# Sixteen weight-sum transfers behind one timing copy in the first projection

## The chip, the cores and the metric

The kernel runs on one core of one Trainium2 chip. The metric is the device time of one execution in microseconds; of several runs the median is given. The core has a matrix engine (TensorE, PE), a vector engine (VectorE, DVE), a scalar engine (ScalarE, ACT), a general engine (GpSimd, POOL) and a queue engine (SyncE, SP) that issues transfers. Each works through its own instructions strictly in order, and waits for the others by semaphores. Transfers are issued from the queues of SP and POOL and carried out by 16 DMA engines.

## The reference

Two layers over 1024 tokens of width 1024, in float32. Each has a token mixer and a SwiGLU channel mixer of width 2816, with RMS norms before them and residual sums behind. Only the first mixer is touched here:

```python
def short_conv_mixer(h, w_in, conv_w, w_out):
    bcx = h @ w_in                          # 1024 x 3072
    b_gate, c_gate, xv = jnp.split(bcx, 3, axis=-1)
    u = b_gate * xv
    y = depthwise causal convolution of u, 3 taps
    return (c_gate * y) @ w_out             # 1024 x 1024
...
x = x + mix
x = x + (silu(g) * u) @ w_down[i]           # g, u = rmsnorm(x) @ w_gate_up[i]
```

## The kernel before

**Products.** Every float32 operand is split into two parts, a rounded one (hi, made by ACT, L1002) and the rest (lo, made by DVE, L1003), and three matmuls take the place of one. Around that lies a scheme with seven products in place of eight: operands and weights are cut into quadrants, sums of quadrants are formed beforehand, and the seven products, numbered k = 0 to 6, are combined by ACT copies and DVE additions. Products 0, 1 and 4 use plain quadrants of the weights; products 2, 3, 5 and 6 use sums of quadrants (s1 to s4).

**The first projection.** It is computed in ten units (`plan_`), each of two blocks of 128 output columns: "bx" units give a column block of b_gate and one of xv, which are multiplied and go through the three taps, and "cc" units give two blocks of c_gate. One product of one unit is a granule of 12 matmuls. Units 0 to 3 (GROUP = 4) go together, product by product, in the order k = 0, 1, 6, 5, 2, 3, 4; their weight sums were stored ahead. Units 4 to 9 ("direct") go one after the other, in the order k = 2, 5, 3, then k = 0 of the next unit, then k = 4, 6, and k = 1 of the next; their weight sums are formed by DVE on the way. In a unit, tile `sa` takes products 0 and 1 in its first half and 2 and 6 in its second, and `s3` takes product 3. ACT copies the first product of each from its accumulator (L600, L611, L618); DVE adds the others (L588) and then multiplies `sa` by `s3` in place (L644); ACT starts the taps (L549) and DVE adds them (L554).

**Weight sums by transfer.** The second product of this mixer (`w_out`) and the first four units of the channel mixer's first product (`w_gu`) need sums of weight quadrants too. Those are formed without any engine: `sums_by_transfer` makes 16 transfers for each, from DRAM to DRAM, 512 KB each; eight copy a quadrant, and eight add another to it on the way (`accum_op`), L992. They are put into one list of 32: eight copies for `out_sums` (tile name s3, printed s_126), eight copies for `first_sums[0]` (s_0_124), eight additions for the first, eight additions for the second. All go out on the queue of POOL. Their readers come later: the second product loads the sums at L1040 and, for some granules, adds them by transfers of its own on POOL (L1070), and POOL stores the residual stream (L842).

**Order of the work.** A helper `Line` holds the matmuls in a row and puts every other step at a due time: `at(t, f)` runs `f` when the row of matmuls reaches `t`. The instructions of each engine go out in that order and stay in it. A transfer from DRAM to DRAM has no operand that is ready late, so by itself POOL would issue it at once. To give it a place, `transfer_behind` (L672) puts a timing copy ahead of it on POOL: it reads one column of a tile that was written at that point of the row, and writes it to an unused column of `cst`. POOL can't go on until that tile is written; and, the other way round, whoever wants to overwrite the tile waits until POOL has read it. The call stands in `unit_product` at L604, and takes a tile by the number of the product.

Of the kernel before, what the change touches and what calls it, by code (L numbers as in the profile page):

```python
# [46 lines left out]
C_ROOM = 368  # L47
# [14 lines left out]
GROUP = 4  # L62
# [12 lines left out]
def trunk_kernel(ctx: ExitStack, tc: tile.TileContext, xT, small, table, w_in, w_out, w_kv, w_q, w_o, w_gu, w_dn, out):  # L75
# [3 lines left out]
    dve, act, pool, pe = nc.vector, nc.scalar, nc.gpsimd, nc.tensor  # L79
# [3 lines left out]
    def slot(tag, shape=(P, D), dtype=F32, bufs=1):  # L83
        uid[0] += 1
        return sb.tile(list(shape), dtype, tag=tag, name=f"{tag}_{uid[0]}", bufs=bufs)
# [136 lines left out]
    cst = slot("cst", (P, C_ROOM))  # L222
# [128 lines left out]
    def conv_layer():  # L351
# [33 lines left out]
        for k in range(NK):  # L385
# [6 lines left out]
            if k < 2 or k % 2 == 0:  # L392
                n = 1 if k < 2 else 2
# [15 lines left out]
        at = line.at  # L409
# [45 lines left out]
        def sources(u):  # L455
            kind, j = plan_[u]
            m1, m2 = (j, 2 * NK + j) if kind == "bx" else (NK + j, NK + j + 1)
            return w_in[m1], w_in[m2]
# [48 lines left out]
        for p in range(4):  # L507
            t = -3.2 + 1.4 * p
            at(t, scale, 0, 2 * p)
            put(0, p, part(p, 0, 0), t + 0.7)  # L510
            t = 10.0 + 1.5 * p
            at(t, scale, 0, 2 * p + 1)
            put(1, p, part(p, 1, 0), t + 0.7)
            t = 18.5 + 1.7 * p
            at(t, scale, 1, 2 * p + 1)
            put(6, p, part(p, 1, 1), t + 0.7)
            t = 27.0 + 3.4 * p
# [3 lines left out]
            t = 39.2 + 2.6 * p  # L521
            at(t, t_sum, t2(p), part(p, 1, 1), part(p, 0, 0))
            put(2, p, t2(p), t + 1.2)
            t = 49.0 + 2.6 * p
            at(t, t_sum, part(p, 0, 1), part(p, 1, 1), part(p, 0, 1))
            put(3, p, part(p, 0, 1), t + 0.7)
            t = 60.0 + 2.6 * p
# [13 lines left out]
        def taps(j, h, u_of, t):  # L541

            w = [cst[:, C_CONV + i * NK + j : C_CONV + i * NK + j + 1] for i in range(NCONV)]
            c = halves[h]

            def first():
                if h == 0:
                    Y[j] = slot(f"X{j}")
                act.activation(Y[j][:, c], u_of()[:, c], AF.Copy, scale=w[2])  # L549

            def add(s):
                a = max(c.start, s)
                y = Y[j][:, a : c.stop]
                dve.scalar_tensor_tensor(y, u_of()[:, a - s : c.stop - s], w[2 - s], y, ALU.mult, ALU.add)  # L554

            at(t, first)
            at(t + 0.8, add, 1)
            at(t + 0.85, add, 2)
# [5 lines left out]
        def unit_product(u, k, tag, direct):  # L564
            kind, j = plan_[u]
            name = {0: "a", 1: "b1", 2: "a", 3: "a", 4: "a", 5: "b", 6: "b" if direct else "b6"}[k]
            get = bank_at(u, name, tag)
            start = k in (0, 1, 5) or k == 6 and not direct
            ops_of = lambda: B[k]
            w1, w2 = sources(u)  # L570
            if not direct:
                src = {0: w1[:, 0], 1: w1[:, 1], 4: w2[:, 1]}
                src = src[k] if k in src else in_sums[u][SUMS[k]]
                ring_granule(4, ops_of, 0, get, start, True, src=src)
            else:
                raw_of = {
                    0: lambda: units[u, "w1"][:, 0],
                    1: lambda: units[u, "w1"][:, 1],
                    4: lambda: units[u, "w2"][:, 1],
                }  # L580
                ring_granule(4, ops_of, 0, get, start, True, raw_of=raw_of.get(k) or (lambda: units[u, "s", k]))
            t = line.end

            def sa(i):
                return units[u, "sa"][:, halves[i]]

            def add(x):
                dve.tensor_tensor(x(), get(), x(), ALU.add)  # L588

            s3 = lambda: units[u, "s3"]  # L590
            flat = lambda: units[u, "sa"]

            def c22():
                dve.tensor_tensor(s3(), units[u, "b"], s3(), ALU.add)

            if k == 0:

                def f():
                    units[u, "sa"] = slot(sa_tags[u])
                    act.copy(sa(0), get())  # L600

                at(t + 0.05, f)
            if (k in (0, 2, 3, 6) if direct else k in (6, 5, 2, 3)):
                at(t + 0.8, lambda: transfer_behind(transfers, s3() if k in (5, 3) else sa(min(k, 1))))  # L604
            if k == 1:
                at(t + 0.05, add, lambda: sa(0))
                if kind == "cc" and direct:
                    at(t + 0.8, gate, j, 0, lambda: sa(0))
            if k == 2:
                if direct:  # L610
                    at(t + 0.05, lambda: act.copy(sa(1), get()))  # L611
                else:
                    at(t + 0.05, add, lambda: sa(1))
            if k == 3 and direct:

                def f():
                    units[u, "s3"] = slot(f"s{u % 2}", (P, HALF))
                    act.copy(s3(), get())  # L618

                at(t + 0.05, f)  # L620
                at(t + 0.75, c22)
                if kind == "cc":
                    at(t + 2.5, gate, j + 1, 1, s3)
            if k == 3 and not direct:
                at(t + 0.05, add, s3)
                if kind == "bx":
                    at(t + 0.8, lambda: dve.tensor_tensor(sa(1), s3(), sa(1), ALU.mult))
            if k == 5 and not direct:

                def f():  # L630
                    if u in (2, 3):
                        units[u, "s3"] = X[2 * u - 2 - 2 * (u == 2)][:, lo_half]
                    else:
                        units[u, "s3"] = slot(f"s{u % 2}", (P, HALF))
                    act.copy(s3(), get())

                at(t + 0.05, f)
                at(t + 0.1, add, lambda: sa(1))
            if k == 6 and not direct:
                at(t + 0.05, lambda: act.copy(sa(1), get()))  # L640
            if k == 6 and direct:
                at(t + 0.05, add, lambda: sa(1))
                if kind == "bx":
                    at(t + 0.8, lambda: dve.tensor_tensor(sa(1), s3(), sa(1), ALU.mult))  # L644
                    taps(j, 1, flat, t + 2.7)
                else:
                    at(t + 0.8, gate, j, 1, lambda: sa(1))
            if k == 4:
                if kind == "bx":
                    at(t + 0.05, lambda: dve.tensor_tensor(sa(0), get(), sa(0), ALU.mult))  # L650
                    taps(j, 0, flat, t + 1.8)
                    if not direct:
                        taps(j, 1, flat, t + (2.5, 8.0, 10.0)[u])
                elif direct:
                    at(t + 0.05, gate, j + 1, 0, get)
                else:
                    c3 = lambda: X[6][:, lo_half]
                    at(t + 0.05, lambda: act.copy(c3(), get()))

                    for h in (0, 1):  # L660
                        at(t + 9.5, gate, j, h, lambda h=h: sa(h))
                        at(t + 12.5, gate, j + 1, h, (c3, s3)[h])

        for k in (0, 1, 6, 5, 2, 3, 4):
            for u in range(GROUP):
                unit_product(u, k, "acc" if k in (0, 2, 3, 4) else f"P{u % 2}", False)
        group_end = line.end
        transfers = sums_by_transfer(out_sums, w_out[0:NK:2], w_out[1:NK:2])
        more = sums_by_transfer(first_sums[0], w_gu[0, 0:GROUP], w_gu[0, NF : NF + GROUP])
        transfers = deque(transfers[:8] + more[:8] + transfers[8:] + more[8:])  # L670

        def transfer_behind(transfers, src):  # L672
            if transfers:
                pool.tensor_copy(cst[:, C_ROOM - 1 :], src[:, 0:1])
                transfers.popleft()()


        def unit_weights(u, t):
# [26 lines left out]
            for i, d in ((1, 5.8), (2, 5.45), (3, 5.2)):  # L705
                at(t - d * unit, lambda i=i: it["f"][i]())

        steady = lambda u, k: unit_product(u, k, {1: "P1", 5: "P0", 6: "P0"}.get(k, "acc"), True)
        steady(GROUP, 0)
        steady(GROUP, 1)  # L710
# [29 lines left out]
        t = group_end  # L740
# [150 lines left out]
    class Line:  # L891
# [8 lines left out]
        def at(self, t, f, *args):  # L900
            self.n += 1
            heapq.heappush(self.heap, (t, self.n, f, args))
# [79 lines left out]
    def sums_by_transfer(dst, w1, w2):  # L982

        rows = lambda ap: ap.rearrange("u p c -> p u c")
        s3, s4, s1, s2 = (rows(dst[:, i]) for i in range(4))
        a11, a12, a21, a22 = (rows(w[:, :, e]) for w in (w1, w2) for e in (0, 1))
        plan = [(s3, a11), (s1, a21), (s2, a22), (s4, a12), (s3, a21), (s1, a22), (s2, s3), (s4, s2)]
        steps = []
        for i, (to, of) in enumerate(plan):
            how = {"accum_op": ALU.add} if i > 3 else {}  # L990
            for h in (slice(0, 2), slice(2, 4)):
                steps.append(lambda to=to[:, h], of=of[:, h], how=how: nc.gpsimd.dma_start(to, of, **how))  # L992
        return steps
# [1481 lines left out]
```

## Time and profile before

| | |
|---|---|
| runs shown | 1896.95, 1896.89, 1899.06 us; median 1896.95 |
| profiled execution | 1898.37 us, span of its instructions 1896.7 us |
| PE | 1878.8 us busy, 99% of the span |
| DVE | 1351.3 us, 71% |
| ACT | 871.9 us, 46% |
| POOL | 377.5 us, 20% |
| DMA | 368.18 MB, mean 194 GB/s |
| granted clock of PE | 0.996 on average |

The times in the rows are microseconds from the start of the span. Lines such as L674 are lines of the kernel before; in the kernel after the change the same statements stand one or two lines lower. In a row of a timeline the number in front is the start, the next the length, and the brackets hold the idle time before it and what ended that. SPq, POOLq and the like are the sequencers of the engines.

### The profile page before, as it was taken

To read this page: it belongs to the slowest core of one execution; us is meant where nothing else is said; L and a number is where in the kernel's file an instruction comes from. 1 tells how busy PE (TensorE), PEld (TensorE's weight loads), DVE (VectorE), ACT (ScalarE), POOL (GpSimd) and SP (SyncE) were. 2 spreads that over 40 slices of the span, in tenths; PEclk is the share of its full clock that TensorE was granted. 3 is DMA by queue.
4 is the path that set the end of the run, shared out by engine and by line. 5 is a ranking of instruction groups with operands and counts; after the bars stand their busy time and mean duration, and the time that the engine had idled before them with its cause. 6 is when DMAs were issued, how large, how long until landed. Compare 5 with 4: busy or idle time off the path is not lost.

```text
span 1896.7 us, 24889 instructions
## 1 busy us (share of the span) xinstructions
PE 1878.8 (99%) x8518; PEld 1560.3 (82%) x8518; DVE 1351.3 (71%) x2197; ACT 871.9 (46%) x1746; POOL 377.5 (20%) x700
## 2 busy tenths in 40 slices
PE   9998999999999999999999999999999999999999
PEld 7886788888888888888888888888888888888887
DVE  8995797868777777676677888567767666765543
ACT  5542356743333334344566777445333333344441
POOL 0132102212222322000015776400111111100000
PEclk9999999999999999999999999999999999999999
DMA  8776657756666666987741114844454654587563
GB/s 311 236 224 154 122 190 190 185 174 205 214 226 221 228 211 213 354 299 267 232 150 32 25 32 150 319 170 143 146 189 150 220 183 163 163 289 258 198 228 102
DMA packets 173312, 368.18 MB, mean 194 GB/s; under 512 B 17216, under 2 KB 63680, under 8 KB 173056
## 3 DMA queue, kind: packets, MB, share of 16 engines
q1 hardware_dynamic: 138240, 255.78, 40.6%
q0 software_dynamic: 34656, 110.64, 18.8%
q8 instruction: 67, 1.10, 0.2%
q14 instruction: 61, 0.50, 0.1%
q10 hardware_dynamic: 288, 0.16, 0.0%
HBM read 261.26 MB, written 115.87 MB: 199 GB/s over the span
## 4 chain that ended last, share of the span: by engine, by line
PE 94%; DVE 3%; issue 2%; POOL 1%; ACT 0%; POOLq 0%; DVEq 0%; ACTq 0%
PE acc L1086 48%; PE P L1086 28%; PE P L1803 2%; PE P L1805 2%; PE P L1804 2%; PE twin L2030 2%; PE acc L179 1%; PE acc L2110 1%; PE P L1212 1%; PE P L1213 1%; PE P L1211 1%; PE acc L1211 1%; PE acc L1212 1%; PE acc L1213 1%; PE acc L2079 1%
## 5 line engine op out<-in xcount | busy, mean ns | idle before, releaser
L1086 PE MATMUL acc<-XS,G 128*128 128x512 f32 x2568 | 607.1, 391 | 13.1 <-ACT G L611 8.6
L1086 PEld LDWEIGHTS acc<-XS,G 128*128 128x128 f32 x2568 | 485.2, 189 | 115.0 <-ACT G L611 9.1
L1086 PE MATMUL acc<-A,G 128*128 128x512 f32 x1674 | 395.4, 389 | 0.0
L1086 PEld LDWEIGHTS acc<-A,G 128*128 128x128 f32 x1674 | 314.3, 188 | 65.3
L1086 PE MATMUL P<-XS,G 128*128 128x512 f32 x1320 | 311.7, 389 | 0.0
L1086 PEld LDWEIGHTS P<-XS,G 128*128 128x128 f32 x1320 | 247.8, 188 | 51.7 <-ACT G L1362 0.2
L1086 PE MATMUL P<-A,G 128*128 128x512 f32 (+1 forms) x1164 | 273.5, 388 | 0.1
L1086 PEld LDWEIGHTS P<-A,G 128*128 128x128 f32 x1164 | 217.8, 188 | 45.5 <-DVE G L588 0.5
L1003 DVE TENSOR_TENSOR G<-WL,G 128x512 fp32r<-128x512 f32 x168 | 115.8, 690 | 78.3 <-ACT G L1002 77.9
L1002 ACT CAST G<-WR 128x512 fp32r<-128x512 f32 (+1 forms) x210 | 126.9, 605 | 66.7 <-PE acc L1086 27.8
L1003 DVE TENSOR_TENSOR G<-WR,G 128x512 fp32r<-128x512 f32 (+1 forms) x210 | 142.2, 677 | 8.7 <-ACT G L1002 8.7
L1002 ACT CAST G<-WH 128x512 fp32r<-128x512 f32 (+1 forms) x168 | 101.1, 602 | 83.0 <-PE acc L1086 31.6
L1002 ACT CAST G<-WL 128x512 fp32r<-128x512 f32 x168 | 103.6, 617 | 68.2 <-DVE WL L924 63.1
L1003 DVE TENSOR_TENSOR G<-WH,G 128x512 fp32r<-128x512 f32 (+1 forms) x168 | 113.3, 674 | 7.2 <-ACT G L1002 7.1
L1362 ACT ACTIVATE G<-G 128x512 f32<-128x512 f32 x48 | 30.4, 632 | 154.5 <-DVE G L1448 154.5
L1559 DVE TENSOR_TENSOR X<-X,acc 128x512 f32<-128x512 f32 x39 | 26.7, 686 | 87.4 <-PE acc L1086 87.4
L951 POOL DMA_DIRECT2D s<-X x48 | 36.6, 763 | 252.2 <-DVE X L926 124.8
L1443 POOL DMA_DIRECT2D h<-X x44 | 24.5, 558 | 251.4 <-DVE X L1440 244.2
L1429 ACT COPY s<-acc 128x512 f32<-128x512 f32 x40 | 23.5, 587 | 98.3 <-PE acc L1086 98.3
L1448 DVE TENSOR_TENSOR G<-P,G 128x512 f32<-128x512 f32 x40 | 27.6, 689 | 42.2 <-PE P L1086 42.2
L1422 DVE TENSOR_TENSOR s<-P,s 128x512 f32<-128x512 f32 x40 | 27.5, 687 | 35.0 <-ACT s L1429 29.3
L1419 ACT COPY G<-acc 128x512 f32<-128x512 f32 x44 | 25.8, 587 | 57.7 <-PE acc L1086 57.7
(329 smaller groups left out, 2730.3 us busy)
## 6 DMA issues: line engine op xcount, KB each, us to landing
G<-h SPq DMA_DIRECT2D x70, 512.0 KB, 5.0
h<-X POOLq DMA_DIRECT2D x44, 512.0 KB, 5.5
X<-in_w_dn SPq DMA_DIRECT2D x80, 256.0 KB, 3.5
s<-X POOLq DMA_DIRECT2D x40, 512.0 KB, 3.8
WR<-in_w_gu SPq DMA_DIRECT2D x36, 512.0 KB, 5.7
WH<-in_w_gu SPq DMA_DIRECT2D x36, 512.0 KB, 6.5
h<-X POOLq DMA_DIRECT2D x66, 256.0 KB, 3.8
WR<-s SPq DMA_DIRECT2D x64, 256.0 KB, 3.4
```

The lines of the kernel that those rows point to most:

```text
L951: nc.gpsimd.dma_start(dst[:, :, c].rearrange("s p c -> p s c"), it["s"])
L1002: lambda: act.copy(out_hi, raw),
L1003: lambda: lo_eng.tensor_tensor(out_lo, raw, plain(out_hi), ALU.subtract),
L1086: pe.matmul(ps, w[:, wp, c], x[:, xp, q], start=first and i == 0, stop=last and i == 2, skip_group_check=True)
L1211: pe.matmul(ps, hi[:, kc], xs[:, 0, c], start=k == 0, stop=False, skip_group_check=True)
L1212: pe.matmul(ps, hi[:, kc], xs[:, 1, c], start=False, stop=False, skip_group_check=True)
L1213: pe.matmul(ps, lo[:, kc], xs[:, 0, c], start=False, stop=k == n_op - 1, skip_group_check=True)
L1362: state["silu"] = act.activation(x, x if of is None else of, AF.Silu, scale=sign)
L1803: pe.matmul(ps, x[:, 0, t], hi, start=k == 0, stop=False)
L1804: pe.matmul(ps, x[:, 0, t], lo, start=False, stop=False)
L1805: pe.matmul(ps, x[:, 1, t], hi, start=False, stop=k == NK - 1)
L2030: pe.matmul(ps, q, k, start=e == 0, stop=e == 1)
```

## The change

Before, each of 32 steps of the projection put one timing copy and one transfer on POOL: products 6, 5, 2 and 3 of units 0 to 3 (16 steps), then products 0, 2, 3 and 6 of the direct units until the list was empty. After, the first 16 steps are as they were. At product 0 of unit 4 one timing copy is followed by all 16 remaining transfers, and the later products of the direct units issue none.

```diff
-            if (k in (0, 2, 3, 6) if direct else k in (6, 5, 2, 3)):
-                at(t + 0.8, lambda: transfer_behind(transfers, s3() if k in (5, 3) else sa(min(k, 1))))
+            if not direct and k in (6, 5, 2, 3):
+                at(t + 0.8, lambda: transfer_behind(s3() if k in (5, 3) else sa(1), 1))
+            if u == GROUP and k == 0:
+                at(t + 0.8, lambda: transfer_behind(sa(0), 16))
...
-        def transfer_behind(transfers, src):
-            if transfers:
-                pool.tensor_copy(cst[:, C_ROOM - 1 :], src[:, 0:1])
+        def transfer_behind(src, n):
+            pool.tensor_copy(cst[:, C_ROOM - 1 :], src[:, 0:1])
+            for _ in range(n):
                 transfers.popleft()()
```

On POOL, in the middle of the direct units, the instructions before are these (tile names with their buffer: G8, G9 and s1 are buffers of `sa` and `s3` tiles, s3_126 and s1_0_124 the weight sums in DRAM; in brackets the semaphores, where DMASW are those of POOL's transfers):

```order
L674 COPY cst_2_64<-G8_218_1423 128x1 [waits Activation_49,Pool_49]
L992 DMA s3_126<-s3_126 128x2x512 [waits DMASW5_49,DMASW1_49]
L674 COPY cst_2_64<-s1_233_1546 128x1 [waits DVE_49,Pool_49]
L992 DMA s3_126<-s3_126 128x2x512 [waits DMASW2_49,DMASW0_49]
L674 COPY cst_2_64<-G9_235_1566 128x1 [waits Activation_49,Pool_49]
L992 DMA s3_126<-s3_126 128x2x512 [waits DMASW3_49,DMASW1_49]
L674 COPY cst_2_64<-G8_218_1423 128x1 [waits DVE_49,Pool_49]
L992 DMA s1_0_124<-in_w_gu 128x2x512
```

After the change the same transfers stand there without copies, from the one copy of unit 4 on to POOL's next own work, the store at L844:

```order
L675 COPY cst_2_64<-G11_206_1316 128x1 [waits Activation_49,Pool_49]
L994 DMA s3_126<-in_w_out 128x2x512 [waits DMASW4_49]
L994 DMA s3_126<-in_w_out 128x2x512 [waits DMASW5_49]
L994 DMA s3_126<-in_w_out 128x2x512 [waits DMASW6_49]
L994 DMA s3_126<-in_w_out 128x2x512 [waits DMASW7_49]
L994 DMA s3_126<-s3_126 128x2x512 [waits DMASW4_49,DMASW0_49]
...
L994 DMA s1_0_124<-s1_0_124 128x2x512 [waits DMASW2_49,DMASW0_49]
L994 DMA s1_0_124<-s1_0_124 128x2x512 [waits DMASW3_49,DMASW1_49]
L844 DMA xres0_108<-A2_301_2076 128x512 [waits DMAHW1_49,DVE_49]
```

The transfers kept their order and their waits for one another; the waits for ACT and DVE between them went.

On DVE nothing is moved, but what an instruction waits for differs. Unit 5, the end of its products 6 and the multiplication of `sa` by `s3`, before:

```order
L588 TENSOR_TENSOR G_218_1423<-P_228_1503,G_218_1423 128x512 [waits PE_49,Pool_49]
L644 TENSOR_TENSOR G_218_1423<-s_233_1546,G_218_1423 128x512 [waits Pool_49]
L1003 TENSOR_TENSOR G_243_1613<-WH_1436,G_243_1613 128x512 [waits Activation_49]
L588 TENSOR_TENSOR G_235_1566<-P_241_1606,G_235_1566 128x512 [waits PE_49]
L554 SCALAR_TENSOR_TENSOR X_239_1597<-G_218_1423,cst_64,X_239_1597 128x512 [waits Activation_49]
```

And after:

```order
L588 TENSOR_TENSOR G_218_1434<-P_228_1510,G_218_1434 128x512 [waits PE_49]
L646 TENSOR_TENSOR G_218_1434<-s_233_1551,G_218_1434 128x512 [waits DVE_49]
L1005 TENSOR_TENSOR G_243_1614<-WH_1445,G_243_1614 128x512 [waits Activation_49]
L588 TENSOR_TENSOR G_235_1569<-P_241_1607,G_235_1569 128x512 [waits PE_49]
L554 SCALAR_TENSOR_TENSOR X_239_1598<-G_218_1434,cst_64,X_239_1598 128x512 [waits Activation_49]
```

The two places where DVE overwrites `sa` no longer wait for POOL.

## The prediction

> **What bounds the kernel now.** I read the page first, then who waits for whom on TensorE (PE), and then the timelines of single engines around the places where PE waits.
>
> ```profile
> span 1896.7 us, 24889 instructions
> PE 94%; DVE 3%; issue 2%; POOL 1%; ACT 0%; POOLq 0%; DVEq 0%; ACTq 0%
> ```
>
> The chain that ended last is PE for 94% of the span: the kernel is a stream of matmuls, and only what leaves PE idle or slow can be won back. The waits of PE in the first projection and the stages behind it, us 60 to 420, are two (group, total us, times, longest us):
>
> ```profile
> PE acc L1086 <- ACT G L611: 8.6, 1, 8.6
> PE acc L1086 <- ACT s L618: 4.5, 1, 4.5
> ```
>
> Their places stand in PE's timeline (start us, length us, the group, and in brackets the idle time before it). The groups here are 12 matmuls, one granule of one unit:
>
> ```profile
> 128.59 2.88 PE L1086 MATMUL acc<-A,G 128*128 128x512 f32 x12
> 131.31 2.88 PE L1086 MATMUL P<-A,G 128*128 128x512 f32 x12
> ...
> 174.83 2.88 PE L1086 MATMUL P<-A,G 128*128 128x512 f32 x12
> 186.36 5.38 PE L1086 MATMUL acc<-XS,G 128*128 128x512 f32 x12 [8.64 <-ACT G L611]
> 191.57 2.89 PE L1086 MATMUL acc<-A,G 128*128 128x512 f32 x12
> ...
> 230.12 2.88 PE L1086 MATMUL acc<-A,G 128*128 128x512 f32 x12
> 237.50 5.40 PE L1086 MATMUL acc<-XS,G 128*128 128x512 f32 x12 [4.50 <-ACT s L618]
> 242.75 2.92 PE L1086 MATMUL P<-XS,G 128*128 128x512 f32 x12
> ...
> 267.27 5.60 PE L1086 MATMUL acc<-A,G 128*128 128x512 f32 x24
> ```
>
> A group takes 131.31 - 128.59 = 2.72 us when nothing is wrong. After each wait the first group takes 191.57 - 186.36 = 5.21 and 242.75 - 237.50 = 5.25 us. The granted clock says why (windows: us, busy of PE, PEld, DVE, ACT, POOL with instructions, then clock, DMA share, GB/s):
>
> ```profile
> 180.00:190.00 10.00, 3.64 (x9) 2.87 (x10) 6.10 (x14) 2.23 (x4) 2.90 (x4) 0.56 0.66 138
> 230.00:240.00 10.00, 5.50 (x20) 4.16 (x19) 7.74 (x13) 2.95 (x6) 2.50 (x3) 0.79 0.49 82
> ```
>
> So an idle PE also loses its clock for a while: 0.56 and 0.79 of full speed over these ten microseconds.
>
> Now what PE waited for, first place, all engines:
>
> ```profile
> 182.49 1.15 POOL L992 DMA_DIRECT2D s<-s  x1 [4.76 <-issue]
> 183.18 0.65 POOL L674 COPY cst<-G 128x1 f32<-128x1 f32 x1
> 183.87 0.69 DVE L644 TENSOR_TENSOR G<-s,G 128x512 f32<-128x512 f32 x1 [13.37 <-POOL cst L674]
> 184.59 0.72 ACT L549 ACTIVATE X<-G,cst 128x512 f32<-128x512 f32 x1 [15.76 <-DVE G L644]
> 185.73 0.57 ACT L611 COPY G<-acc 128x512 f32<-128x512 f32 x1
> ...
> 186.36 2.08 PE L1086 MATMUL acc<-XS,G 128*128 128x512 f32 x4 [8.64 <-ACT G L611]
> ```
>
> Read it upwards. PE waits for ACT to empty an accumulator (L611). ACT stands in its own order behind the first tap (L549), which waits for VectorE (DVE). DVE's multiplication L644 overwrites a tile, and waits 13.37 us because a timing copy on POOL (L674), which only reads one column of that tile, has not run. The copy stands behind a transfer that POOL could not issue before 182.49. The second place has the same shape:
>
> ```profile
> 231.50 0.66 POOL L674 COPY cst<-G 128x1 f32<-128x1 f32 x1
> 232.19 0.69 DVE L588 TENSOR_TENSOR G<-P,G 128x512 f32<-128x512 f32 x1 [10.36 <-POOL cst L674]
> ...
> 236.87 0.58 ACT L618 COPY s<-acc 128x512 f32<-128x512 f32 x1
> ```
>
> All waits of DVE for POOL between 120 and 260 are these, with a third one, of 16.4 - 13.4 = 3.0 us at L644, that cost PE nothing:
>
> ```profile
> DVE G L644 <- POOL cst L674: 16.4, 2, 13.4
> DVE G L588 <- POOL cst L674: 10.4, 1, 10.4
> ```
>
> POOL is late because of a rate. From the timeline of POOL:
>
> ```profile
> 132.31 0.18 POOL L674 COPY cst<-G 128x1 f32<-128x1 f32 x1 [11.79 <-ACT G L600]
> 132.90 1.22 POOL L992 DMA_DIRECT2D s<-in_w_out  x1 [0.41 <-issue]
> ...
> 236.90 1.15 POOL L992 DMA_DIRECT2D s<-s  x1 [4.74 <-issue]
> ```
>
> Sixteen accumulating transfers go out between 132.90 and 236.90, one per 104.0 / 15 = 6.93 us. A steady unit issues four of them and has seven granules on PE, 7 x 2.72 = 19.0 us; four transfers need 27.7 us. POOL falls 8.7 us behind per unit, and its copies, which hold tiles that DVE wants to overwrite, fall behind with it.
>
> **The change, part by part.** Removed: 15 timing copies of the steady units. Their own POOL time (0.65 us each by the rows above, some 10 us) lies between transfers that POOL waits for anyway: price nothing. Kept: the 16 copies of the first four units, one copy of the steady units, which runs as before at 132.31, right after its tile is written, and all 32 transfers in the same order. Moved: transfers 17 to 32 no longer wait for later tiles. PE, DVE, ACT and SP keep their instructions in the same order; what goes is the wait for POOL on the DVE rows at L588 and L644.
>
> The gain: every group start from 128.59 to 267.27 is one of 44 groups of 12. At 2.72 us they need 119.68 us, and they took 138.68. The difference, **19.0 us**, is everything PE loses here: waits 8.64 + 4.50, slow groups 5.21 - 2.72 = 2.49 and 5.25 - 2.72 = 2.53, and 0.84 of smaller lateness behind the stalls. With the POOL waits gone I take all of it. Profiled: 1898.37 - 19.0 = 1879.4 us for that execution (span 1896.7, 1.7 around it). The median of the runs shown, 1896.95, lies 1.4 below the profiled execution, so on its scale 1877.95. I add 0.2 for small stalls: **1878.2 us**.
>
> The Trainium skill ("TensorE: Matmul & The Clock Gate", Part 1) says that PE falls to half clock after an idle window of about 3.4 us and needs about 3.4 us of sustained work to get back. By this estimate each stall costs 1.7 us beyond its wait, and the sum would be 19.0 - (5.02 - 3.4) = 17.4 us, 1879.6. The trace agrees on the halving, but shows 2.5 us per stall, and the rows decide.
>
> Three prices can't be read directly. First, the pace of the transfers without the copies between them. POOL issued the last one 4.74 us after its copy had ended, so the transfer before it set the time, not the copy; I take 6.93 us as it is. Nothing below excludes a faster pace, but no one waits for these transfers yet (the third price), so it brings nothing; above, the slowest lies here (median us from issue to landing, one transfer in us 159 to 170):
>
> ```profile
> s<-s POOLq DMA_DIRECT2D x1, 512.0 KB, 10.4
> ```
>
> Second, DVE. Freed of its waits it has this much work in the dense stretch behind the first one:
>
> ```profile
> 183.90:216.00 32.10, 29.52 (x118) 23.91 (x119) 31.78 (x52) 12.41 (x22) 5.89 (x8) 0.88 0.74 154
> ```
>
> It was busy 31.78 of 32.10 us there, catching up. Without the wait the same work starts at 183.87 - 13.37 = 170.5; PE's schedule of the stretch moves by 8.64 + 2.49 = 11.1, so its end at 216 becomes 204.9, and DVE has 34.4 us for 31.8. It fits, with 2.6 to spare: between 0 and some 5 us of stall if it bunches badly; I take 0.
>
> Third, the readers of the transfers and what shares the DMA engines:
>
> ```profile
> 247.06 0.80 SPq L761 DMA_DIRECT2D A<-in_xT  x2
> 260.27 0.68 DVE L828 TENSOR_TENSOR A<-A,acc 128x512 f32<-128x512 f32 x1
> 263.38 0.33 SPq L1040 DMA_DIRECT2D WR<-s  x1
> 277.67 0.62 POOL L842 DMA_DIRECT2D xres<-A  x1 [39.62 <-DVE A L828]
> 300.31 0.89 POOL L1070 DMA_DIRECT2D G<-s  x1 [13.40 <-DVE A L1003]
> ```
>
> PE's work arrives 19 us earlier, the transfers do not. The sums of w_out are first read at 263.38 - 19 = 244; the transfer that finishes them is the eighth, about 132.9 + 8 x 6.93 = 188. POOL's next own work, the stores at 277.67 - 19 = 259, meets a queue that is free at about 132.9 + 16 x 6.93 = 244. Both have 15 us or more to spare. Tightest are the inputs that are loaded again at L761, in a burst (queue: packets, MB, share of 16 engines in us 246 to 262; then KB each and median us to landing):
>
> ```profile
> q1 hardware_dynamic: 1674, 5.12, 85.0%
> A<-in_xT SPq DMA_DIRECT2D x8, 512.0 KB, 6.8
> ```
>
> Today the burst has the engines to itself. Then it starts at 228, with two or three transfers (6.93 us each) still to come. The first pair lands at about 247.06 + 6.8 = 253.9 and is added at 260.27: 6.4 us to spare. I take 0; the other end is what the first rival below costs.
>
> **The rivals.**
>
> *Late loads.* The burst, 0.85 x 16 = 13.6 us of all engines, shares 16 us with transfers that hold about half of them by themselves (0.49 in the row 230:240, where little else moves), some 8 us more: 21.6 us of work for 16, so it ends 5.6 us later. DVE and ACT, in order, wait for a late tile, and some 5 us reach PE: 1878.2 + 5 = 1883. For it: only 6.4 us of slack; against it: the later tiles have more. The Trainium skill ("DMA: Bandwidth & Descriptors", Queues, rings and completion order) says that each DMA engine goes round-robin, packet by packet, between the queues; by that rule the loads are slowed as here. Chance 0.08.
>
> *DVE becomes the bound.* It bunches by up to 5 us: 1883. For it the 31.78 of 32.10; against it the 2.6 us left. Chance 0.05.
>
> *One stall stays.* If ACT at the second place was held by something else than DVE's wait, 4.50 + 2.53 = 7.0 us stay: 1885. The 10.36 row speaks against. Chance 0.03.
>
> *The change doesn't do what it says*, PE still waits for the transfers in another way, and the time stays at 1897. The rows L588 and L644 speak against. Chance 0.02.
>
> *Slower: POOL's queue reaches the next stage.* With p us per transfer, POOL is free at 132.9 + 16p, does four stores of about 0.6 us, and comes to the lo transfer of L1070 that feeds PE, wanted at 300.31 - 19 = 281.3. The code asks for it 11.8 us ahead of PE (LEAD 13.0 less 1.2), and it lands in about 6 (the transfers of L1070 before 330):
>
> ```profile
> DMA to landing us min/median/max: 4.0/5.9/6.4
> ```
>
> So PE stalls 132.9 + 16p + 2.4 - 281.3 - 5.8 = 16p - 151.8 us. That eats the whole 19.0 from p = 10.7 on; at p = 11.5 it is 32 and the time 1897 - 19 + 32 = 1910. The slowest single one took 10.4, so all would have to be slower than that. Chance 0.02.
>
> **How the numbers follow.** Forecast 0.80, late loads 0.08, DVE 0.05, one stall 0.03, no change 0.02, slower 0.02. The forecast's own range is 1876.5 to 1880.5, from the 2.2 us by which the runs shown differ among themselves. The range must hold 8 in 10 and take in the bounds of the unknown costs, so up to 1885: 1876.5 to 1885. About 0.2% (3.8 us) is what a measurement of this kernel can tell from no change; forecast and the first three rivals are faster than that: 0.96, less a little for what I have not thought of: 0.94, same 0.03, slower 0.03.
>
> **What would show it.** In the changed profile, right: no wait of DVE for POOL between 120 and 260; no PE wait for L611 or L618; the granted clock 1.00 in every window from 120 to 260; the granule that started at 267.27 starts at about 248.3; the transfers still end around 240 to 245, at some 6.9 us each. Wrong, and where: a wait of DVE L828 or ACT for a DMA between 228 and 262 is the late loads; DVE full with PE waiting between 170 and 205 is the DVE bound; a wait in front of L1070 on POOL until after 282 is the slower case. The forecast is wrong if PE's stalls stay with DVE no longer waiting for POOL.

## The result, and the profile after

The changed kernel takes 1879.51 us (median of 4 runs, 1879.20 to 1879.86), the kernel before 1897.86 us (median of 4, 1896.89 to 1899.06). The ratio is 0.9903, with a 95% interval of 0.9886 to 0.9920: faster by 18.4 us, about 1%. The profiled span went from 1896.7 to 1877.6 us, 19.1 less.

The page of the changed kernel has PE at 99% of the chain that ended last, where it was 94%:

```profile
span 1877.6 us, 24850 instructions
PE 1873.0 (100%) x8518; PEld 1556.6 (83%) x8518; DVE 1352.1 (72%) x2197; ACT 872.4 (46%) x1746; POOL 372.0 (20%) x685
PE 99%; DVE 1%; ACT 0%; issue 0%
```

Of the waits of PE (group, total us, times, longest us) over the whole span one is left, at the start of the kernel; those for L611 (now L613) and L618 (now L620) are gone:

```profile
PE P L377 <- DVE s L374: 1.1, 1, 1.1
```

PE's timeline of the stage shows the same groups one after the other every 2.72 us, without a gap:

```profile
128.44 2.88 PE L1088 MATMUL acc<-A,G 128*128 128x512 f32 x12
...
174.68 2.88 PE L1088 MATMUL P<-A,G 128*128 128x512 f32 x12
177.40 2.88 PE L1088 MATMUL acc<-XS,G 128*128 128x512 f32 x12
180.12 2.88 PE L1088 MATMUL acc<-A,G 128*128 128x512 f32 x12
...
248.12 5.60 PE L1088 MATMUL acc<-A,G 128*128 128x512 f32 x24
```

From 128.44 to 248.12 are 119.68 us, exactly 44 groups of 2.72; before it took 138.68. That is the whole difference of the spans but for 0.1 us at the start.

POOL's timeline (start, length, in brackets the idle time before) shows that the transfers themselves didn't get faster. They go out at 132.75 to 241.59, (241.59 - 132.75) / 15 = 7.26 us apart, where it was 6.93:

```profile
132.15 0.18 POOL L675 COPY cst<-G 128x1 f32<-128x1 f32 x1 [10.99 <-ACT G L600]
132.75 1.22 POOL L994 DMA_DIRECT2D s<-in_w_out  x1 [0.41 <-issue]
140.04 1.16 POOL L994 DMA_DIRECT2D s<-in_w_out  x1 [6.07 <-issue]
...
231.34 1.16 POOL L994 DMA_DIRECT2D s<-s  x1 [4.99 <-issue]
241.59 1.15 POOL L994 DMA_DIRECT2D s<-s  x1 [9.09 <-issue]
259.06 0.62 POOL L844 DMA_DIRECT2D xres<-A  x1 [16.33 <-DVE A L830]
```

What changed is who stands behind them: after the copy at 132.15 nothing on POOL that another engine waits for, until the store at 259.06. Between the last two lie 10.25 us, where it was 6.09: the inputs are now loaded again beside it. In a view of the DMA (KB each, median us to landing) in us 227 to 244 the landing of these inputs went from 6.8 to 8.7 us, and ACT waits for two weight loads (group, total us, times, longest us), which it does not in the kernel before:

```profile
A<-in_xT SPq DMA_DIRECT2D x8, 512.0 KB, 8.7
...
ACT G L1004 <- DMA WR<-in_w_out: 1.2, 1, 1.2
ACT G L1004 <- DMA WH<-in_w_out: 1.0, 1, 1.0
```

Neither reaches PE.

DVE's busy time in the dense stretch came out as the working had it: 31.98 us of work in 34.50 us (window, us, busy of PE, PEld, DVE, ACT, POOL, then clock, DMA share, GB/s), and the clock stays full, here and in every window of 10 us from 120 to 260:

```profile
170.40:204.90 34.50, 34.50 (x154) 28.58 (x153) 31.98 (x53) 12.42 (x22) 5.84 (x6) 1.00 0.68 145
```

### The profile page after: what moved, and what is told of

Read it like the earlier page. It is cut to its first block, busy times and chain, and to the rows that moved or that the text cites. A ratio compares the mean times of both kernels' runs of the same rounds, so it can differ in the third digit from the quotient of the medians.

```text
span 1877.6 us, 24850 instructions
## 1 busy us (share of the span) xinstructions
PE 1873.0 (100%) x8518; PEld 1556.6 (83%) x8518; DVE 1352.1 (72%) x2197; ACT 872.4 (46%) x1746; POOL 372.0 (20%) x685
## 3 DMA queue, kind: packets, MB, share of 16 engines
q0 software_dynamic: 34656, 110.64, 18.8%
## 4 chain that ended last, share of the span: by engine, by line
PE 99%; DVE 1%; ACT 0%; issue 0%
PE acc L1088 50%; PE P L1088 30%; PE P L1805 2%; PE P L1807 2%; PE P L1806 2%; PE twin L2032 2%; PE acc L179 1%; PE acc L2112 1%; PE P L1214 1%; PE P L1215 1%; PE P L1213 1%; PE acc L1215 1%; PE acc L1213 1%; PE acc L1214 1%; PE acc L2081 1%; PE acc L183 1%
## 5 line engine op out<-in xcount | busy, mean ns | idle before, releaser
L1005 DVE TENSOR_TENSOR XS<-G,XS 128x1024 fp32r<-128x1024 f32 (+1 forms) x38 | 42.6, 1122 | 14.1 <-ACT XS L1004 14.0
```

The lines of the kernel that those rows point to most:

```text
L1005: lambda: lo_eng.tensor_tensor(out_lo, raw, plain(out_hi), ALU.subtract),
```

## The experiments

The theory: a timing copy costs nothing by itself and a transfer costs nothing by itself; what costs is that a copy in POOL's queue *holds a tile* for as long as POOL is late, and POOL is late because four transfers don't fit into a unit. The rivals: the copies themselves cost; the order or the run of the transfers matters; every copy costs a little.

### Copies that hold nothing

The kernel before, with all copies and transfers in their places. Each copy of the direct units reads a column that ACT or (for k = 6) DVE wrote for it, in place of the tile itself:

```diff
-                at(t + 0.8, lambda: transfer_behind(transfers, s3() if k in (5, 3) else sa(min(k, 1))))
+                at(t + 0.8, lambda: transfer_behind(transfers, s3() if k in (5, 3) else sa(min(k, 1)), (dve if k == 6 else act) if direct else None))
...
-        def transfer_behind(transfers, src):
+        column = [C_EPS + 1]
+
+        def transfer_behind(transfers, src, eng):
             if transfers:
-                pool.tensor_copy(cst[:, C_ROOM - 1 :], src[:, 0:1])
+                src = src[:, 0:1]
+                if eng is not None:
+                    mark = cst[:, column[0] : column[0] + 1]
+                    column[0] += 1
+                    if eng is act:
+                        act.copy(mark, src)
+                    else:
+                        dve.tensor_copy(mark, src)
+                    src = mark
+                pool.tensor_copy(cst[:, C_ROOM - 1 :], src)
                 transfers.popleft()()
```

> The kernel before with all its 32 timing copies and the same place of every transfer on POOL; the only difference is what the copies of the direct units read: a column of their own, written for each by ACT (products 0, 2, 3) or DVE (product 6) from the tile that they read before. So POOL still waits for the same moment, but no longer holds a tile that DVE wants to overwrite. Theory (the copies cost time only by holding sa tiles behind a late POOL): DVE waits no longer for POOL, both PE stalls go, about 1879.5 us, up to 1881 with the 16 small writes. Rival (what counts is that the transfers go out in one run, or that POOL is freed of copies): as before, 1897 to 1898, with PE idle by some 13 us.

Measured: 1879.62 us (1879.35 to 1880.13, 4 runs), ratio 0.9904 (0.9887 to 0.9920). Between 120 and 260 DVE never waits for POOL. The decisive place is the first stall; on DVE it reads:

```profile
169.86 0.69 DVE L588 TENSOR_TENSOR G<-P,G 128x512 f32<-128x512 f32 x1
170.58 0.15 DVE L683 COPY cst<-G 128x1 f32<-128x1 f32 x1
170.77 0.69 DVE L644 TENSOR_TENSOR G<-s,G 128x512 f32<-128x512 f32 x1
```

L644 starts at 170.77, where it started at 183.87. POOL, though, is later than in either kernel, with copies between all transfers and the last of them out at 250.30:

```profile
241.18 1.16 POOL L1003 DMA_DIRECT2D s<-s  x1 [9.69 <-issue]
241.87 0.72 POOL L685 COPY cst<-cst 128x1 f32<-128x1 f32 x1
250.30 1.15 POOL L1003 DMA_DIRECT2D s<-s  x1 [7.70 <-issue]
258.68 0.62 POOL L853 DMA_DIRECT2D xres<-A  x1 [7.24 <-DVE A L839]
```

So the run of transfers isn't what wins, nor the missing copies: here a late POOL costs nothing as long as it holds no tile.

### Copies without transfers

The kernel before with its copies, without the 16 accumulating transfers, so that the weight sums stay incomplete and only the time is of use:

```diff
                 pool.tensor_copy(cst[:, C_ROOM - 1 :], src[:, 0:1])
-                transfers.popleft()()
+                step = transfers.popleft()
+                if len(transfers) >= 16:
+                    step()
```

> The kernel before with all its timing copies, but the last 16 transfers (the accumulating ones) are left out, so the weight sums of the second product and of the channel mixer's first units are incomplete and the output isn't the reference's. Theory (the copies alone cost nothing; they cost what POOL is late behind the transfers): 1879.0 to 1880 us, no wait of DVE for POOL over 1 us. Rival (the copies themselves, or their waits for ACT and DVE, cost the time): 1897.

Measured: 1879.62 us (1879.50 and 1879.74), ratio 0.9903 (0.9883 to 0.9923). What is left of the waits of DVE for POOL:

```profile
DVE G L644 <- POOL cst L674: 0.7, 2, 0.3
```

The same copies on the same tiles are free when POOL isn't late.

### One copy put back, unit 5

The changed kernel, with the run cut in two:

```diff
             if u == GROUP and k == 0:
-                at(t + 0.8, lambda: transfer_behind(sa(0), 16))
+                at(t + 0.8, lambda: transfer_behind(sa(0), 8))
+            if u == GROUP + 1 and k == 6:
+                at(t + 0.8, lambda: transfer_behind(sa(1), 8))
```

> The changed kernel with one timing copy put back: the run of 16 is cut into two of 8, the second behind a copy that reads product 6 of unit 5 (where the kernel before had the copy of its first stall). Theory (one held tile is enough): the copy stands behind the eighth transfer of the run, issued at 183.1, and reads its tile at about 183.9; DVE wants to overwrite that tile at about 170.4 and waits 13.4 us; of that 8.8 reach PE, and 2.5 more by the low clock: 1879.5 + 11.3 = 1890.8 us, one PE wait for L613. Rival (the loss is spread over the 15 copies, some 1.3 us each): 1880.8.

Measured: 1891.42 us (1891.14 to 1892.64, 5 runs), 11.9 more than the changed kernel where 11.3 were expected. The place, with this one copy, is the image of the kernel before with its 15:

```profile
182.51 1.15 POOL L996 DMA_DIRECT2D s<-s  x1 [4.87 <-issue]
183.20 0.65 POOL L677 COPY cst<-G 128x1 f32<-128x1 f32 x1
183.88 0.69 DVE L648 TENSOR_TENSOR G<-s,G 128x512 f32<-128x512 f32 x1 [13.31 <-POOL cst L677]
...
185.74 0.58 ACT L615 COPY G<-acc 128x512 f32<-128x512 f32 x1
...
186.37 2.07 PE L1090 MATMUL acc<-XS,G 128*128 128x512 f32 x4 [8.58 <-ACT G L615]
```

On PE the stall costs 8.58 and a slow group, 190.63 - 186.37 - 2.72 = 1.54 us (1.0 less than before); then two groups come late, because DVE catches up, 196.65 - 193.37 - 2.72 = 0.56 and 205.48 - 202.23 - 2.72 = 0.53:

```profile
186.37 4.42 PE L1090 MATMUL acc<-XS,G 128*128 128x512 f32 x12 [8.58 <-ACT G L615]
190.63 2.89 PE L1090 MATMUL acc<-A,G 128*128 128x512 f32 x12
193.37 2.88 PE L1090 MATMUL acc<-XS,G 128*128 128x512 f32 x12
196.65 3.02 PE L1090 MATMUL P<-XS,G 128*128 128x512 f32 x12 [0.40 <-DVE s L594]
...
202.23 2.88 PE L1090 MATMUL acc<-XS,G 128*128 128x512 f32 x12
205.48 3.01 PE L1090 MATMUL P<-A,G 128*128 128x512 f32 x12 [0.38 <-DVE G L588]
```

That the total came within 0.6 us is partly luck: the 2.5 us expected for the clock were 1.0 too many, and the 1.1 us of catching up were not in the sum at all.

### One copy put back, unit 8

```diff
             if u == GROUP and k == 0:
-                at(t + 0.8, lambda: transfer_behind(sa(0), 16))
+                at(t + 0.8, lambda: transfer_behind(sa(0), 15))
+            if u == GROUP + 4 and k == 0:
+                at(t + 0.8, lambda: transfer_behind(sa(0), 1))
```

> The changed kernel with one other copy put back: 15 transfers in a run, then a copy that reads product 0 of unit 8 (where the kernel before had the copy of its second stall), then the last transfer. Theory (the lateness of POOL at the copy sets the price, and stalls don't add, because the first stall gave POOL time): the copy reads at about 232.0; DVE wants its tile at about 210.2 and waits some 22 us; less 5.8 us that PE has in hand (10.36 - 4.5 in the kernel before) and with 2.5 for the clock that is 18.5: 1898.0 us, as slow as the kernel before with 15 copies more. Rival (this copy costs what the second stall cost, 4.5 + 2.5): 1886.5. Rival (1.3 us per copy): 1880.8.

Measured: 1898.27 us (1897.37 to 1900.13, 8 runs), ratio to the kernel before 1.0004 (0.9993 to 1.0014); 1898.0 was expected. One timing copy of 0.66 us costs as much as all fifteen:

```profile
231.51 0.66 POOL L677 COPY cst<-G 128x1 f32<-128x1 f32 x1
232.20 0.69 DVE L588 TENSOR_TENSOR G<-P,G 128x512 f32<-128x512 f32 x1 [22.40 <-POOL cst L677]
...
237.51 0.79 PE L1090 MATMUL acc<-XS,G 128*128 128x512 f32 x1 [16.39 <-ACT s L622]
```

DVE waits 22.40 us, where 22 were expected, and 16.39 of them reach PE. The next group starts at 241.80, so the first one lost 241.80 - 237.51 - 2.72 = 1.57 us, where 2.5 were expected. The two single copies together cost 11.9 + 18.8 = 30.7 us, the kernel before only 18.4 more than the changed one: stalls on one lateness don't add. POOL reaches this copy at 231.51, in the kernel before at 231.50; but there the first stall had moved PE and DVE 12 us back already, so DVE waited 10.36 and not 22.40 us.

### Three transfers per unit

The kernel before, in the direct units without the step behind product 6:

```diff
-            if (k in (0, 2, 3, 6) if direct else k in (6, 5, 2, 3)):
+            if (k in (0, 2, 3) if direct else k in (6, 5, 2, 3)):
```

> The kernel before with its paired copies and transfers, but in the direct units only behind products 0, 2 and 3 and no longer behind 6: three transfers per unit in place of four, the same 16 in all, the last at unit 9. Theory (a matter of rates: four transfers of some 6.9 us don't fit into a unit of 19.0 us, and the lateness grows): three need 20.8 us, POOL falls only 1.8 us behind per unit and some 9 in all, which the 8 to 13 us between a tile's copy and its overwriting cover nearly: 1879.5 to 1882. Rival (any chain of copies behind transfers holds DVE up): 1890 or more.

Measured: 1880.49 us (1879.38 and 1881.59), ratio 0.9915 (0.9886 to 0.9943). DVE waits for POOL twice, 1.7 us at the longest, and in the profiled execution, the faster of the two, nothing of it reaches PE:

```profile
DVE G L588 <- POOL cst L674: 3.2, 2, 1.7
```

The copy at product 0 of unit 8, which made the second stall of the kernel before at 231.50, still stands on POOL and now runs 20.8 us sooner:

```profile
210.71 0.64 POOL L674 COPY cst<-G 128x1 f32<-128x1 f32 x1
```

So the gain is also to be had with 15 copies more, at a rate that nearly fits: the last of the 16 transfers goes out at 240.97, one per (240.97 - 132.89) / 15 = 7.21 us, so three take 21.6 us and POOL still falls behind a little. This kernel speaks for the rate at the second stall alone: the copy of the first one, behind product 6, is not in it.

### All 32 in one run

```diff
-            if not direct and k in (6, 5, 2, 3):
-                at(t + 0.8, lambda: transfer_behind(s3() if k in (5, 3) else sa(1), 1))
-            if u == GROUP and k == 0:
-                at(t + 0.8, lambda: transfer_behind(sa(0), 16))
+            if u == 0 and k == 6:
+                at(t + 0.8, lambda: transfer_behind(sa(1), 32))
```

> The changed kernel with no timing copies left but one: all 32 transfers in a run behind a copy that reads product 6 of unit 0 (the place of the first copy before). Theory (the first 16 copies cost nothing, since POOL kept up there): 1879.5 us, the transfers end some 10 us sooner and before the inputs are loaded again at about 228. Rival (those copies spread the 16 plain transfers, 8 MB, among the weight loads of units 0 to 3; in a run they make the loads late): PE waits between 80 and 125, 1882 or more.

Measured: 1880.41 us (1879.16 and 1881.66), ratio 0.9914 (0.9885 to 0.9943). The profiled one of the two has a span of 1880.0; its waits of PE lie before the first of these transfers, at the start of the kernel (L377, L179), and its first timing copy already comes at 79.85, 2.2 us later than in the changed kernel (77.61). Behind that nothing stalls PE, and the other run was as fast as the changed kernel. The last transfer goes out at 221.88 in place of 241.59, before the inputs are loaded again (19.7 us sooner, where some 10 were expected):

```profile
79.85 0.20 POOL L673 COPY cst<-G 128x1 f32<-128x1 f32 x1 [21.32 <-ACT G L640]
...
221.88 1.15 POOL L992 DMA_DIRECT2D s<-s  x1 [4.83 <-issue]
```

So the first sixteen need no copies to space them either. No gain over the changed kernel can be told.

### The run begun later

Two kernels put the run behind product 0 of unit 6 and of unit 7. This is the one for unit 6; the other has GROUP + 3:

```diff
-            if u == GROUP and k == 0:
+            if u == GROUP + 2 and k == 0:
                 at(t + 0.8, lambda: transfer_behind(sa(0), 16))
```

> The changed kernel with its run of 16 begun two units later, behind product 0 of unit 6, at about 170. By the formula of the prediction's slower case, POOL is free at 170.8 + 16p, does four stores and comes to the first transfer that feeds PE, wanted at 281.3 with 5.8 us in hand: with p = 6.9 nothing reaches PE, with p = 7.3 (the mean pace of the changed kernel) 3 us and the low clock after it: 1879.5 to 1885. Rival (POOL's queue isn't on the path there, or PE has more in hand): 1879.5. Rival (the reloaded inputs and weights come late, since the transfers now run beside all of them): PE waits between 228 and 270, 1885 or more.

> The same with the run behind product 0 of unit 7, at about 190. By the formula POOL is free at 189.9 + 16p, 301 (p = 6.9) to 307 (p = 7.3), and PE stalls 16 to 22 us near 290 to 310, with up to 2.5 for the clock: 1895.5 to 1904. Here the run costs what it gains elsewhere. Rival (POOL's queue isn't on the path there): 1879.5 to 1882.

Measured: behind unit 6 1879.42 us (1879.24 and 1879.59), ratio 0.9909 (0.9880 to 0.9938); behind unit 7 1890.51 us (1887.34 to 1893.77, 5 runs), ratio 0.9964 (0.9945 to 0.9982). The run of unit 7 in POOL's timeline, and the one wait of PE that it makes:

```profile
184.43 1.22 POOL L994 DMA_DIRECT2D s<-in_w_out  x1
...
291.70 1.15 POOL L994 DMA_DIRECT2D s<-s  x1 [5.77 <-issue]
292.38 2.18 POOL L844 DMA_DIRECT2D xres<-A  x3
299.38 0.56 POOL L844 DMA_DIRECT2D xres<-A  x1 [4.81 <-DVE s L846]
299.92 1.81 POOL L1072 DMA_DIRECT2D G<-s  x2
```

```profile
PE P L1088 <- DMA G<-s: 8.5, 1, 8.5
```

The mechanism of the prediction's slower case exists: POOL's queue reaches the transfers that feed PE. Its price was too high: 16 to 22 us of stall were expected, and the time lies below the expected 1895.5 to 1904. I had the run begin at 189.9, and it began at 184.43, because the units' first products are not 19.0 us apart at the beginning (the copies of units 4, 6 and 7 ran at 132.15, 164.53 and 183.84). And PE had more in hand: the transfer of L1072 was issued at 299.92 and not at 282.95 as in the changed kernel, 17.0 us late, and PE waited 8.5, so it had 8.4 us in hand there, not 5.8. Not all of the 17.0 us is POOL's time on the run: behind it the fourth store stood for 4.81 us, and the profile names DVE L846, which writes a tile that this store doesn't touch, so what held it stays open. Behind unit 6 the first one went out at 284.64, 1.7 us late, and PE didn't notice.

## Why the prediction was right, point by point

- **The chain.** PE waits for ACT, ACT for DVE, DVE for a copy on POOL, the copy for a transfer: shown. With the tiles free and every copy and transfer kept, the waits are gone and the time is that of the changed kernel; with one tile held again, a wait is back.
- **The rate.** Four transfers of 6.93 us against 19.0 us of a unit: shown by copies without transfers, and for the second stall by three per unit.
- **The gain.** 19.0 us from the 44 groups against 19.1 in the spans. In its parts, waits and slow groups, it went as worked out.
- **The 1878.2.** Measured 1879.51, 1.3 more. The step that was off is the last: the sum on the scale of the profiled execution, 1898.37 - 19.0 = 1879.4, was right within 0.2, and I moved it down by 1.4 to the median of three runs. More runs of the kernel before have medians of 1897.86 (4), 1897.96 (16) and 1897.60 (6), so the 1896.95 was on the low side. The 0.2 for small stalls was not needed.
- **The price of the transfers.** Taken as 6.93 us each, unchanged; it became 7.26. Of the 4.8 us more over the whole run, 4.2 lie between the last two transfers (10.25 in place of 6.09), beside the loads of the inputs from 227.9 on. With one copy at unit 8, where these loads begin at 246.1, the same two lie 6.13 apart, which speaks for the loads as the cause. The last one goes out at 241.6 and not at 236.9, with 16 us to spare before POOL's next work.
- **Late loads.** The rival's first half happened: landing 8.7 us in place of 6.8, ACT waits 1.2 and 1.0 us. Its second half, PE waiting, did not, also not with the run begun 32 us later.
- **DVE as the bound.** 31.98 us of work in 34.50, no wait of PE. How near it is shows the unit 5 experiment, where a DVE that is 13 us late costs PE about 1.1 us more while it catches up.
- **The slower case.** It doesn't happen in the change, but as a formula it was mis-sized in several terms, which the run of unit 7 shows. With its pace, (291.70 - 184.43) / 15 = 7.15 us, the formula gives 189.9 + 114.4 + 2.4 - 281.3 - 5.8 = 19.6 us of stall for the 8.5 measured. The run began 5.5 us earlier. POOL went on 0.7 us after the last transfer had gone out and not a whole 7.15 (6.5 less). The four stores took 299.92 - 292.38 = 7.5 us and not 2.4 (5.1 more). The first transfer that feeds PE is issued at 282.95 in the changed kernel and not at 281.3 (1.7 less), and PE has 8.4 us in hand and not 5.8 (2.6 less).

## What to carry to other kernels

A copy that only marks a moment is a reader of its tile: whoever overwrites that tile waits for the queue in which the copy stands, with all that stands ahead of it. So compare the rate at which paced work is added to a queue with the rate at which the queue drains, and let the mark read something that nobody overwrites, or issue the work in one run, as long as the queue is empty before its next work is due. A stall has no fixed price per copy: one copy behind a late queue can cost what fifteen cost, so removing a part of them may bring nothing.

## What the runs showed of the hardware that I had not expected

- **What an idle PE costs beyond its wait differs between runs.** The first group after a wait lost 2.49 and 2.53 us in the kernel before (waits 8.64 and 4.50), but 1.54 us with one copy at unit 5 (wait 8.58) and 1.57 us with one at unit 8 (wait 16.39). So the price doesn't follow the length of the wait: 8.64 and 8.58 differ by 1 us in what comes after. In windows over the first group after the stall, the kernel before has the clock at 0.50 through all of it, and the unit 5 kernel at 0.64:

```profile
186.30:191.50 5.20, 5.14 (x12) 4.08 (x13) 5.17 (x13) 1.14 (x3) 1.56 (x2) 0.50 0.74 160
```

```profile
186.40:190.60 4.20, 4.20 (x12) 3.39 (x13) 4.17 (x12) 1.02 (x2) 1.15 (x1) 0.64 0.67 182
```

  The estimate of 1.7 us that the prediction worked out from the Trainium skill ("TensorE: Matmul & The Clock Gate", Part 1), and set aside for the 2.5 of the trace, lies between these measurements. When the clock fell to 0.50 and when it was full again can be read from windows of 0.1 us. A mean of 0.68 in us 181.20 to 181.30, for example, is a full clock up to 181.24 and half of it from there on:

```profile
181.20:181.30 0.10, 0.00 (x0) 0.00 (x0) 0.00 (x0) 0.00 (x0) 0.00 (x0) 0.68 1.22 225
191.40:191.50 0.10, 0.10 (x2) 0.10 (x1) 0.10 (x1) 0.00 (x0) 0.00 (x0) 0.62 0.53 82
```

  All five stalls, read in this way (in us):

| stall | clock falls | PE works again | clock full | half clock lasts | first group loses |
|---|---|---|---|---|---|
| before, first | 181.24 | 186.36 | 191.48 | 10.24 | 2.49 |
| before, second | 235.85 | 237.50 | 242.68 | 6.83 | 2.53 |
| one copy, unit 5 | 182.58 | 186.37 | 189.41 | 6.83 | 1.54 |
| one copy, unit 8 | 223.55 | 237.51 | 240.62 | 17.07 | 1.57 |
| run from unit 7 | 302.25 | 306.25 | 309.08 | 6.83 | no whole group |

  The loss is half the time from PE's first matmul to the full clock: 5.12, 5.18, 3.04 and 3.11 us make 2.56, 2.59, 1.52 and 1.55. And the half clock lasted 3, 2, 2, 5 and 2 times 3.41 us, as if it changed only at the ends of steps of that length; in the kernel before the two falls, too, lie 54.61 us = 16 such steps apart. So what a stall costs hangs on where in a step PE comes back. With PE back 0.37, 0.31 and 0.59 us into a step the clock was full at its end, with PE back 1.71 and 1.65 us into it only a step later. Five stalls show this; where between 0.59 and 1.65 us it turns, they don't.
- **Accumulating transfers from DRAM to DRAM went out one at a time.** Sixteen in a row without anything between them left POOL 5.9 to 11.1 us apart in the changed kernel, about as long as one takes to land (5.6 to 10.8 us, median 6.4). The plain ones in the run of 32 took 4.3 to 10.1 us to land, median 7.2, but left it 2.4 us apart, (115.82 - 80.00) / 15, by these rows:

```profile
80.00 2.08 POOL L992 DMA_DIRECT2D s<-in_w_out  x3
...
115.82 0.69 POOL L992 DMA_DIRECT2D s<-in_w_gu  x1 [2.35 <-issue]
```

  Why POOL holds an accumulating one back so long was not tried: it may be one of its waits for earlier transfers (DMASW in the lists of the change) or the queue itself.
